# Experts' weights in rows of 8 and 4 KB, the residual in the matching channel order, and a held-back sum

## The chip, the cores and the metric

The kernel runs on one core of one Trainium2 chip, in one launch. The metric is the device time in microseconds (us). A core has five engines that run beside each other: TensorE (PE, matrix products into the PSUM banks, with its weight loads listed as PEld), VectorE (DVE), ScalarE (ACT), GpSimd (POOL) and SyncE (SP, which here issues the DMAs). [...]

## What is computed

One layer of a hybrid diffusion block on 512 latent tokens and 256 context tokens of 2048 channels, all in float32. Ahead of the part that matters here stand a modulated norm, one input projection, three kinds of heads and the output projection w_out with the gated residual. Then:

```python
hl = _rmsnorm(xl, g_ffn) * (1.0 + s2_l) + sh2_l
f = _hier_moe(hl, ...)        # top-1 of 4 groups, top-2 of its 8 experts; 32 experts
#   per expert e:  (silu(h @ w1[e]) * (h @ w3[e])) @ w2[e],  w1, w3: 2048 x 512,  w2: 512 x 2048
xl = xl + ga2_l * f
return _rmsnorm(xl, g_final)
```

The weights of one expert are three matrices of 4.19 MB; all 32 experts' are read once.

## The kernel before, in words

The whole program up to the end of the experts is in an order written out by hand: each engine works through its instructions in program order, and a tile's buffer is given out again once its last reader in program order has been issued. PSUM has eight banks (line 57): four with the tag `mm`, which from line 1205 on are the `held` banks for the rest of the kernel, and four with the tag `bg`, from which `bank()` takes one for a short time.

**The residual.** `out_tile` (line 868) finishes one of 16 tiles of 128 channels of the output projection: DVE adds the gated residual, TensorE transposes the tile (`xtr`) and adds to the router's logits, ACT copies the transposed tile into `xr` (128 tokens on the partitions, 4 token tiles, 2048 channels in natural order) and takes the squares. The last tile (line 886) shares this between ACT and DVE.

**The experts** go in 16 pairs (`expert_pair`, line 1385), two experts side by side in the two column halves of TensorE. `gather` (line 1308) fetches the tokens of four experts, so of two pairs: it splits `xr` into high and low parts (`token_parts`, ACT copies, DVE subtracts), multiplies them with a one-hot matrix in 16 steps (four channel groups of four token tiles; the fourth step of a group is followed by four DVE evacuations `hg`, line 1348, and the next group's first step writes the same two `held` banks). The steps are dealt out over the second pair of each four experts by `STEPS` (line 43), through `steps(n)`.

In a pair, w1 and w3 are multiplied in four column groups of four channel tiles each; behind the first group stands what is in `late`. Then DVE multiplies the two results (line 1427), TensorE transposes them (`pt`), ACT copies them (`at`), and `down` multiplies with w2 in four runs of 512 columns, each into one `held` bank, alternating. After each run DVE scales it (`ys`, line 1451), `split` makes a high and a low part (ACT line 128, DVE line 129), and `combine` (line 1370) is put in `late`: for four token tiles, two products into a bank `pc`, and a DVE addition into the running residual `xf` (line 1381). It runs behind the next run's products, the last run's behind the first group of the next pair's w1.

**The weights.** `wseq` lists tiles of 1 MB in the order of use: two channel tiles of both experts for w1 and w3, two row tiles of both experts and 512 columns for w2, all in rows of 2 KB, each tile by two DMAs of 512 KB (line 1113). SP issues them as buffers come free; in the steady state there are ten (six of `wpool`, one of `moe`, three of `mixs`). `next_w` gives back the tile used before, issues what fits, and takes the next.

Of the kernel before, what the change touches and what calls it, by code (L numbers as in the profile page):

```python
# [50 lines left out]
def hybrid_block_kernel(ctx: ExitStack, tc: tile.TileContext, I, out):  # L51
# [419 lines left out]
    def cc(c):  # L471
        return slice(128 * c, 128 * c + 128)
# [395 lines left out]
    def out_tile(dt, po):  # L868

        xt = ob["xt"].pop(dt)  # L870
        if dt == KT - 1:
            nc.scalar.copy(ob["logs"][0][TWO[0]], pl["log"][TWO[0]])
        nc.vector.scalar_tensor_tensor(xt, po, ga1[:, dt:dt + 1], xt, op0=ALU.mult, op1=ALU.add)
        yield
        if dt == 0:
            pl["log"] = bank("plog")
        pt = bank("xtr")
        for t in range(4):
            nc.tensor.transpose(pt[:, cc(t)], xt[:, cc(t)], ident)
        waiting.append((dt, xt))  # L880
        while waiting and (dt % 2 or dt == KT - 2):
            k, x_ = waiting.popleft()
            sl = TWO[k % 2]
            nc.tensor.matmul(pl["log"][sl], ob["wrs"][:, k], x_, start=k < 2, stop=k >= KT - 2,
                             tile_position=(0, sl.start))
        if dt == KT - 1:

            rows = pt.rearrange("p (t d) -> p t d", t=4)
# [3 lines left out]
            nc.vector.tensor_copy(xr[:, 2:4, cc(dt)], rows[:, 2:4])  # L892
            for t in (2, 3):
                x_ = xr[:, t, cc(dt)]
                nc.vector.tensor_tensor_reduce(sqs[t], x_, x_, 1.0, 0.0, op0=ALU.mult, op1=ALU.add,
                                               accum_out=ob["ssq"][:, t, dt:dt + 1])
            nc.scalar.copy(ob["logs"][0][TWO[1]], pl["log"][TWO[1]])
            nc.scalar.copy(xr[:, 0:2, cc(dt)], rows[:, 0:2])
            return
        nc.scalar.copy(xr[:, :, cc(dt)], pt.rearrange("p (t d) -> p t d", t=4))  # L900
        for t in range(4):
            sq = ob["pool"].tile([P, P], F32, name="sq", tag="sq", bufs=4)
            nc.scalar.activation(sq, xr[:, t, cc(dt)], AF.Square, accum_out=ob["ssq"][:, t, dt:dt + 1])
            if t == 1:
                yield
        yield
# [99 lines left out]
    def four(which, name, dtype=F32):  # L1006

        return mixs.tile([P, 4, 512], dtype, name=name, tag=f"m{which}")

    def split_mix(*at):  # L1010

        for n in at:
            q, m = n // 4, MIX_ORDER[n]
            if n % 4 == 0:
                halves[q] = [four(2 * q + j, "mx", F32R) for j in range(2)]
            mh[m], ml[m] = (t[:, n % 4] for t in halves[q])
            nc.scalar.copy(mh[m], mix[m])
            (nc.gpsimd if 4 <= n < 15 else nc.vector).tensor_tensor(ml[m], mix[m], mh[m].bitcast(F32), op=ALU.subtract)  # L1018

    def open_out():  # L1020
# [39 lines left out]

        ob["constant"] = constant()

    def load_xt(dt):
        xt = ob["xt"][dt] = ob["pool"].tile([P, T], F32, name="xt", tag="xt", bufs=6)
        nc.sync.dma_start(xt, I["xT"][dt])


    def rows(t, k, n):

        return t[:, 0:2 * k * n // 512].rearrange("p a (b n) -> p (a b) n", n=n).rearrange("p (e k) n -> p e k n", e=2)  # L1070

    wseq = deque()

    def add(name, e, k, nk, o, n):
        v = I[name][e:e + 2].rearrange("e (k p) n -> p e k n", p=P)
        wseq.append((nk, n, v[:, :, k:k + nk, o:o + n]))

    for e in range(0, NE, 2):
        for name in ("w1", "w3"):
            for k in range(0, KT, 2):  # L1080
                add(name, e, k, 2, 0, 512)
        for c in range(4):
            if e < NE - 2 or c < 3:
# [15 lines left out]
    def load_weights(n=1000):  # L1099
        while places and wseq and n:  # L1100
            n -= 1
            at = places.popleft()
            if at not in until or total - len(wseq) < until[at]:
                nk, c, v = wseq.popleft()
                if at == "w":
                    w = ob["wpool"].tile([P, 4, 512], F32, name="w", tag="w")
                elif at == "m":
                    w = moe.tile([P, 4, 512], F32, name="wm", tag="wm")
                else:
                    w = four(at, "w")  # L1110
                w = rows(w, nk, c)
                for j in range(2):
                    nc.sync.dma_start(w[:, j], v[:, j])
                wtiles.append((w, at))

    def next_w():

        places.extend(used)
        used.clear()
        load_weights()  # L1120
        w, at = wtiles.popleft()
        used.append(at)
        return w

    def beside_out(i, n):
        run(jobs, n)
# [177 lines left out]
    def prod():  # L1304
        turn.rotate()
        return turn[0]

    def gather(g):
# [12 lines left out]
        for n in range(16):  # L1321
# [22 lines left out]
            if t == 3:  # L1344
                for i in range(4):
                    k = 4 * c + i
                    h = moe.tile([P, 256], F32, name="hg", tag="hg", bufs=16)
                    nc.vector.scalar_tensor_tensor(h, pg[i], A2[:, k:k + 1], norm, op0=ALU.mult, op1=ALU.mult)
                    nc.scalar.activation(h, h, AF.Identity, bias=B2[:, k:k + 1])  # L1349
                    hs.append(h)  # L1350
            yield

    xf = {}
    late = deque()
    fs = keep.tile([P, 4, 5], F32, name="fs")

    def square(t, i, x):
# [11 lines left out]

    def combine(oht, c, o, n, hl, last=False, ts=range(4)):  # L1370

        x = xf.get(c)
        if x is None:
            x = xr[:, :, 512 * c:512 * c + 512]
            xf[c] = four(1 + c, "xf")
        for t in ts:
            pc = bank("pc")
            for m, y in enumerate(hl):
                nc.tensor.matmul(pc[:, 0:n], oht[:, cc(t)], y[:, 0:n], start=m == 0, stop=m == 1)  # L1379
            x_ = xf[c][:, t, o:o + n]  # L1380
            nc.vector.tensor_tensor(x_, pc[:, 0:n], x[:, t, o:o + n], op=ALU.add)  # L1381
            if last:
                square(t, c + o // 256, x_)

    def expert_pair(e, oh, hs):
        last = e == NE - 2
# [3 lines left out]
        for name in ("w1", "w3"):  # L1390
            acc = prod()
            for c in range(4):
                if name == "w1" and e == 0:

                    steps(FIRST[c])
                for k in range(4 * c, 4 * c + 4):
                    if k % 2 == 0:
                        w = next_w()
                    for j in range(2):
                        nc.tensor.matmul(acc[64 * j:64 * j + 64], hs[k][:, sl + 64 * j:sl + 64 * j + 64], w[:, j, k % 2],  # L1400
                                         start=k == 0, stop=k == KT - 1, tile_position=(0, 64 * j))
# [46 lines left out]
        def scaled(pd, c, o, n):  # L1448
# [2 lines left out]
            nc.vector.scalar_tensor_tensor(ys, pd, tw[:, 1:2], ga2b[:, 512 * c + o:512 * c + o + n], op0=ALU.mult, op1=ALU.mult)  # L1451
            return ys

        if not last:
# [79 lines left out]
    with tc.If(flag > 0):  # L1534
# [3 lines left out]
        hT = ov.tile([P, KT, T], F32, name="hT")  # L1538
        for t in range(4):
            y = big([D], "y")  # L1540
            nc.scalar.mul(y, xr[:, t], rst[:, t:t + 1])
# [171 lines left out]
```

## Time and profile before

| | |
|---|---|
| median of 3 runs | 2288.06 us (2285.24 to 2288.96) |
| the profiled execution | 2293.04 us |
| its span, first to last instruction | 2291.3 us |
| its granted clock, mean | 0.99 |
| TensorE busy / DVE / ACT / POOL | 96% / 54% / 30% / 12% |
| DMA moved | 600.81 MB, mean 262 GB/s |

Up to about 1230 us run the projections and heads, from about 1248 to 2272 us the experts, then the last norm and the store. The busy shares are means over stages of different kinds, so the stretch of the experts is read by itself, in windows. A wait is idle time of an engine, put down to what ended it. The DMA share can pass 1, since packets of one engine overlap.

### The profile page before, as it was taken

Reading aid. Unit: us, or ns where it says so; the run is one execution under the profiler, and the core shown is the slowest. Engines: PE = TensorE matmul, PEld = TensorE weight load, DVE = VectorE, ACT = ScalarE, POOL = GpSimd, SP = SyncE. Lnnn points to the kernel's source line nnn. Section 1 sums busy time; section 2 is a strip of 40 time slices with the busy share of each in tenths; the row PEclk is TensorE's granted clock in tenths of the full one; section 3 lists DMA queues with packets and bytes.
Section 4 is the critical chain, followed back from the end, with each engine's and each line's share of the span. In section 5 each row is a group of like instructions: output and inputs, shape, how many; then the busy total and the mean of one; then the engine's idle time right before and its main releaser. Section 6 shows DMA issues by size and latency. Waiting matters only on the chain. (4 is left out here: it accounts for less than half of the span.)

```text
span 2291.3 us, 32501 instructions
## 1 busy us (share of the span) xinstructions
PE 2191.1 (96%) x12151; PEld 1414.7 (62%) x12151; DVE 1245.8 (54%) x2201; ACT 692.4 (30%) x1400; POOL 268.3 (12%) x323
## 2 busy tenths in 40 slices
PE   7989999999999999999998999999999999999996
PEld 4667888888877887877776444444435344444433
DVE  4468668868777666645555333434434343434424
ACT  4344232332444445452334121211202021211202
POOL 0033414405122121122000000000000000000000
PEclk9999999999999999999999999999999999999998
DMA  9964222222346555536974999999999999999996
GB/s 342 370 205 138 75 92 70 84 88 86 112 147 176 174 174 164 167 93 200 303 262 168 328 344 369 403 380 404 381 404 382 390 403 380 403 381 404 381 404 261
DMA packets 321234, 600.81 MB, mean 262 GB/s; under 512 B 25392, under 2 KB 35376, under 8 KB 321072
## 3 DMA queue, kind: packets, MB, share of 16 engines
q1 hardware_dynamic: 317232, 593.44, 72.3%
q0 software_dynamic: 3840, 5.25, 1.1%
q8 instruction: 97, 1.59, 0.3%
q14 instruction: 65, 0.53, 0.1%
HBM read 589.15 MB, written 4.19 MB: 259 GB/s over the span
## 5 line engine op out<-in xcount | busy, mean ns | idle before, releaser
L209 PE MATMUL p<-xh,wh 128*128 128x512 f32 (+1 forms) x1184 | 417.0, 365 | 4.3 <-ACT wh L128 2.1
L1400 PE MATMUL held<-w,hg 128*64 128x512 f32 x1848 | 416.2, 596 | 1.2 <-ACT hg L1349 0.6
L210 PE MATMUL p<-xl,wh 128*128 128x512 f32 (+1 forms) x1184 | 399.5, 354 | 0.0
L1400 PEld LDWEIGHTS held<-w,hg 128*64 128x64 f32 x1848 | 126.8, 137 | 239.2 <-issue 214.1
L129 DVE TENSOR_TENSOR wl<-w,wh 128x512 fp32r<-128x512 f32 x216 | 176.5, 817 | 160.4 <-ACT wh L128 144.8
L212 PE MATMUL p<-xh,wl 128*128 128x512 f32 (+1 forms) x1184 | 254.2, 352 | 5.6 <-DVE wl L129 5.6
L209 PEld LDWEIGHTS p<-xh,wh 128*128 128x128 f32 x1184 | 223.9, 189 | 46.1 <-issue 5.6
L210 PEld LDWEIGHTS p<-xl,wh 128*128 128x128 f32 x1184 | 224.1, 189 | 34.1 <-issue 1.4
L128 ACT CAST wh<-w 128x512 fp32r<-128x512 f32 x216 | 133.6, 619 | 317.4 <-PE p L210 219.1
L1444 PE MATMUL held<-w,at 128*64 128x512 f32 (+1 forms) x944 | 213.6, 595 | 10.9 <-ACT at L1434 10.9
L212 PEld LDWEIGHTS p<-xh,wl 128*128 128x128 f32 x1184 | 191.4, 189 | 35.1 <-DVE wl L129 7.9
L1381 DVE TENSOR_TENSOR xf<-pc,xf 128x512 f32<-128x512 f32 (+1 forms) x244 | 149.6, 674 | 50.9 <-PE pc L1379 50.8
L1191 DVE TENSOR_TENSOR parts<-xr,parts 128x512 fp32r<-128x512 f32 x112 | 76.9, 691 | 167.8 <-ACT parts L1190 167.8
L1332 PEld LDWEIGHTS held<-oh,parts 128*128 128x128 f32 x896 | 111.5, 188 | 67.2 <-issue 46.9
L369 DVE SCALAR_TENSOR_TENSOR m_acc<-w_ada,sc,m_acc 128x512 f32<-128x512 f32 x180 | 145.5, 809 | 10.7 <-DMA w_ada<-w_ada 8.4
L1444 PEld LDWEIGHTS held<-w,at 128*64 128x64 f32 x944 | 63.1, 137 | 128.5 <-issue 104.2
L1332 PE MATMUL held<-oh,parts 128*128 128x256 f32 x896 | 128.4, 289 | 14.4 <-ACT hg L1349 10.3
L1190 ACT CAST parts<-xr 128x512 fp32r<-128x512 f32 x112 | 68.5, 618 | 167.5 <-PE held L1332 166.6
L128 ACT CAST wh<-ys 128x512 fp32r<-128x512 f32 x60 | 37.1, 618 | 255.2 <-DVE ys L1451 147.5
L209 PE MATMUL po<-mx,wh 128*128 128x512 f32 x256 | 105.3, 411 | 2.3 <-ACT wh L128 1.6
L1379 PE MATMUL pc<-wh,oht 128*128 128x512 f32 (+1 forms) x260 | 105.7, 407 | 0.0
L210 PE MATMUL po<-mx,wh 128*128 128x512 f32 x256 | 102.9, 402 | 0.3 <-DVE mx L1018 0.2
(359 smaller groups left out, 2823.5 us busy)
## 6 DMA issues: line engine op xcount, KB each, us to landing
w<-w SPq DMA_DIRECT2D x692, 512.0 KB
w_ada<-w_ada SPq DMA_DIRECT2D x384, 256.0 KB
w<-w_in SPq DMA_DIRECT2D x184, 256.0 KB
wm<-w SPq DMA_DIRECT2D x74, 512.0 KB
w<-w_out SPq DMA_DIRECT2D x64, 256.0 KB
w_st<-w_st SPq DMA_DIRECT2D x32, 192.0 KB
x<-xT SPq DMA_DIRECT2D x16, 256.0 KB
xt<-xT SPq DMA_DIRECT2D x16, 256.0 KB
```

The source lines that it names most:

```text
L128: nc.scalar.copy(wh, w)
L129: nc.vector.tensor_sub(wl, w, wh.bitcast(F32))
L209: nc.tensor.matmul(po, h, mh_, start=first, stop=False)
L210: nc.tensor.matmul(po, h, ml_, start=False, stop=False)
L212: nc.tensor.matmul(po, l, mh_, start=False, stop=last)
L369: nc.vector.scalar_tensor_tensor(accs[j], loads.popleft(), s, accs[j], op0=ALU.mult, op1=ALU.add)
L1191: engine.tensor_tensor(l, x_, h.bitcast(F32), op=ALU.subtract)
L1332: nc.tensor.matmul(pg[i], y[:, cc(i)], oh[:, t], start=t == 0 and m == 0 and i % 2 == 0, stop=t == 3 and m == 1 and i % 2 == 1)
L1379: nc.tensor.matmul(pc[:, 0:n], oht[:, cc(t)], y[:, 0:n], start=m == 0, stop=m == 1)
L1381: nc.vector.tensor_tensor(x_, pc[:, 0:n], x[:, t, o:o + n], op=ALU.add)
L1400: nc.tensor.matmul(acc[64 * j:64 * j + 64], hs[k][:, sl + 64 * j:sl + 64 * j + 64], w[:, j, k % 2], start=k == 0, stop=k == KT - 1, tile_p ...
L1444: nc.tensor.matmul(pd[64 * j:64 * j + 64, 0:n], at[:, 128 * f + 64 * j:128 * f + 64 * j + 64], w[:, j, f - f0], start=f == 0, stop=f == 3, ...
```

## The change

1. w1 and w3 are read expert by expert in runs of 512 channels: partition p takes the four consecutive rows 4p to 4p + 3, one row of 8 KB in HBM, a whole tile of 1 MB in one DMA. So channel tile i of a run now holds the channels 4p + i. w2 is read in tiles of one row tile, both experts, 1024 columns: rows of 4 KB.
2. The residual `xr` is written in that order (`spread`), so the gather's parts have the matching channels; the first addition of each column run puts it back in natural order (`in_order`), as does the branch for overflowing tokens. The shift and gain are permuted once, by 16 small products with columns of the identity.
3. `next_w(2)` takes both experts' tiles at once. `down_two` multiplies two column runs beside each other: runs 0 and 1 in the `held` banks, runs 2 and 3 in two `bg` banks. The gather's steps of two runs follow each other. The last pair keeps `down`.
4. Behind each of the first column groups at most one entry of `late` runs. The combination of run 3 goes to `fill` and is done at the next pair's change from w3 to w2: two token tiles ahead of the transposes and two behind them.

The core of the diff:

```diff
-        nc.scalar.copy(xr[:, :, cc(dt)], pt.rearrange("p (t d) -> p t d", t=4))
+        for t in range(4):
+            nc.scalar.copy(spread(dt)[:, t], pt[:, cc(t)].rearrange("p (q i) -> p i q", i=4))
...
+        pq = bank("pq")
+        for m in range(4):
+            for i in range(4):
+                nc.tensor.matmul(pq[32 * m:32 * m + 32, 0:2 * KT].rearrange("p (w g i) -> p w g i", w=2, i=4)[:, :, :, i],
+                                 ident[:, i::4], mods[:, 3:5, m::4, 0], start=True, stop=True, tile_position=(0, 32 * m))
+        nc.vector.tensor_copy(mods[:, 3:5, :, 1], pq[:, 0:2 * KT].rearrange("p (w k) -> p w k", w=2))
...
+    def add_run(name, e, c):
+        wseq.append((0, 0, I[name][e, 512 * c:512 * c + 512].rearrange("(p k) n -> p k n", p=P)))
...
-            for k in range(0, KT, 2):
-                add(name, e, k, 2, 0, 512)
+            for c in range(4):
+                for j in range(2):
+                    add_run(name, e + j, c)
+        if e < NE - 2:
+            for c in (0, 2):
+                for k in range(4):
+                    add("w2", e, k, 1, 512 * c, 1024)
+            continue
...
+            if (c, t) not in begun:
+                begun.add((c, t))
+                natural = lambda y: y.rearrange("p (q i) -> p q i", i=4)
+                nc.vector.tensor_tensor(natural(x_), natural(pc), in_order(xr[:, t, 512 * c:512 * c + 512]), op=ALU.add)
+            else:
+                nc.vector.tensor_tensor(x_, pc[:, 0:n], x_, op=ALU.add)
...
+                ws = next_w(2)
...
-                while late:
+                if late:
                     late.popleft()()
...
         nc.vector.tensor_mul(a, gu[1], a)
+        filler((0, 1))
...
         nc.scalar.copy(at, pt)
+        filler((2, 3))
...
+        def down_two(c0):
+            pds = [prod(), prod()] if not c0 else [bank("pd"), bank("pd")]
+            for f in range(4):
+                w = next_w()
+                for pd, cs in zip(pds, (slice(0, 512), slice(512, 1024))):
+                    for j in range(2):
+                        nc.tensor.matmul(pd[64 * j:64 * j + 64], at[:, 128 * f + 64 * j:128 * f + 64 * j + 64],
+                                         w[:, j, 0, cs], start=f == 0, stop=f == 3, tile_position=(0, 64 * j))
+            return pds
...
-            for c in range(4):
-                pd = down(c, 0, 512)
+            for c0 in (0, 2):
+                pds = down_two(c0)
                 if ahead:
-                    steps(STEPS[6 + c])
+                    steps(STEPS[6 + c0] + STEPS[7 + c0])
                 while late:
                     late.popleft()()
-                hl = split(scaled(pd, c, 0, 512))
-                late.append(lambda ts=range(4), c=c, hl=hl: combine(oht, c, 0, 512, hl, ts=ts))
+                for c, pd in zip((c0, c0 + 1), pds):
+                    hl = split(scaled(pd, c, 0, 512))
+                    if c < 3:
+                        late.append(lambda c=c, hl=hl: combine(oht, c, 0, 512, hl))
+                    else:
+                        fill.append(lambda ts, hl=hl: combine(oht, 3, 0, 512, hl, ts=ts))
```

## Rows read from the trace of the kernel before

**Rows 1.** The page, part 1: busy us (share of the span) x instructions.
```profile
PE 2191.1 (96%) x12151; PEld 1414.7 (62%) x12151; DVE 1245.8 (54%) x2201; ACT 692.4 (30%) x1400; POOL 268.3 (12%) x323
```

**Rows 2.** Windows: PE, PEld, DVE, ACT, POOL busy us (instructions), clock, DMA share, GB/s.
```profile
1510.00:1520.00 10.00, 10.00 (x53) 5.81 (x53) 7.00 (x12) 0.87 (x2) 0.00 (x0) 1.00 0.99 349
...
1550.00:1560.00 10.00, 10.00 (x45) 4.10 (x42) 5.28 (x8) 1.23 (x2) 0.00 (x0) 1.00 1.05 408
1529.50:1657.81 128.31, 123.59 (x610) 57.41 (x608) 52.22 (x94) 24.19 (x45) 0.00 (x0) 1.00 1.04 393
```

**Rows 3.** TensorE's waits, 1255 to 2245 us: us in total, times, longest.
```profile
PE pt L1432 <- DVE act L1427: 10.9, 16, 0.9
PE held L1332 <- ACT hg L1349: 10.3, 7, 1.5
PE held L1444 <- ACT at L1434: 10.2, 15, 0.7
PE held L1332 <- DVE parts L1191: 4.1, 14, 0.3
PE held L1400 <- ACT hg L1349: 0.6, 1, 0.6
PE held L1400 <- DMA w<-w: 0.6, 2, 0.3
```

**Rows 4.** Timeline at a change to w2: start, us, engine, line [idle before].
```profile
1544.58 0.69 DVE L1427 TENSOR_TENSOR act<-held,act 128x512 f32<-128x512 f32 x1 [13.06 <-PE held L1400]
1545.33 0.66 PE L1432 MATMUL pt<-cf,act 128*128 128x128 f32 x4 [0.87 <-DVE act L1427]
1546.02 0.58 ACT L1434 COPY at<-pt 128x512 f32<-128x512 f32 x1 [15.81 <-PE pt L1432]
1546.66 7.09 PE L1444 MATMUL held<-w,at 128*64 128x512 f32 x32 [0.68 <-ACT at L1434]
```

**Rows 5.** Timeline of one combination behind a w2 run.
```profile
1553.68 0.50 PE L1379 MATMUL pc<-wh,oht 128*128 128x512 f32 x1
1554.02 0.39 PE L1379 MATMUL pc<-wl,oht 128*128 128x512 f32 x1
1554.25 0.40 PE L1379 MATMUL pc<-wh,oht 128*128 128x512 f32 x1
1554.45 2.48 DVE L1381 TENSOR_TENSOR xf<-pc,xf 128x512 f32<-128x512 f32 x4 [1.91 <-PE pc L1379]
...
1555.72 1.94 PE L1444 MATMUL held<-w,at 128*64 128x512 f32 x8
```

**Rows 6.** Timeline of gather steps 11 (1619.72) and 12 (1624.44).
```profile
1619.72 1.20 PE L1332 MATMUL held<-oh,parts 128*128 128x256 f32 x8
1620.85 0.62 ACT L1190 CAST parts<-xr 128x512 fp32r<-128x512 f32 x1 [4.76 <-PE held L1332]
1620.86 3.65 PE L1444 MATMUL held<-w,at 128*64 128x512 f32 x16
...
1622.11 1.65 DVE L1348 SCALAR_TENSOR_TENSOR hg<-held,mods,norm 128x256 f32<-128x256 f32 x4
...
1624.44 1.21 PE L1332 MATMUL held<-oh,parts 128*128 128x256 f32 x8
...
1625.49 0.39 PE L1379 MATMUL pc<-wh,oht 128*128 128x512 f32 x1
```

**Rows 7.** Timeline of the output projection's end.
```profile
1221.98 0.56 ACT L900 COPY xr<-xtr 128x512 f32<-128x512 f32 x1
...
1224.38 1.05 PE L884 MATMUL plog<-xt,wrs 128*36 128x512 f32 x2 [1.13 <-ACT logs L872]
```

**Rows 8.** An ACT copy of 128 columns out of PSUM: ns min/median/max.
```profile
L379 ACT COPY rows<-sums x16: 243/266/273, 236.8 to 1197.8; 128x128 f32<-128x128 f32 x16
```

**Rows 9.** Timeline: eight small instructions of TensorE.
```profile
1197.29 0.43 PE L376 MATMUL sums<-m_acc,cf 128*32 128x128 f32 x8
```

**Rows 10.** Timeline: a strided reduction; line 1381: the first additions, ns.
```profile
1063.35 1.18 DVE L1054 TENSOR_REDUCE ws<-wr 128x36 f32<-128x576 f32 x1
...
L1381 DVE TENSOR_TENSOR xf<-pc,xr x16: 680/681/692, 1297.7 to 1316.4; 128x512 f32<-128x512 f32 x16
```

More of the change, by code (lines that the diff above doesn't have):

```diff
@@ L886, in out_tile @@
         if dt == KT - 1:
-            rows = pt.rearrange("p (t d) -> p t d", t=4)
+            rows, to = pt.rearrange("p (t q i) -> p t i q", t=4, i=4), spread(dt)
             sqs = [ob["pool"].tile([P, P], F32, name="sq", tag="sq", bufs=4) for _ in range(4)]
@@ L891, in out_tile @@
                 nc.scalar.activation(sqs[t], pt[:, cc(t)], AF.Square, accum_out=ob["ssq"][:, t, dt:dt + 1])
-            nc.vector.tensor_copy(xr[:, 2:4, cc(dt)], rows[:, 2:4])
             for t in (2, 3):
-                x_ = xr[:, t, cc(dt)]
-                nc.vector.tensor_tensor_reduce(sqs[t], x_, x_, 1.0, 0.0, op0=ALU.mult, op1=ALU.add,
+                nc.vector.tensor_copy(to[:, t], rows[:, t])
+            for t in (2, 3):
+                x_ = to[:, t]
+                nc.vector.tensor_tensor_reduce(sqs[t].rearrange("p (i q) -> p i q", i=4), x_, x_, 1.0, 0.0, op0=ALU.mult, op1=ALU.add,
                                                accum_out=ob["ssq"][:, t, dt:dt + 1])
             nc.scalar.copy(ob["logs"][0][TWO[1]], pl["log"][TWO[1]])
-            nc.scalar.copy(xr[:, 0:2, cc(dt)], rows[:, 0:2])
+            for t in (0, 1):
+                nc.scalar.copy(to[:, t], rows[:, t])
             return
-        nc.scalar.copy(xr[:, :, cc(dt)], pt.rearrange("p (t d) -> p t d", t=4))
+        for t in range(4):
+            nc.scalar.copy(spread(dt)[:, t], pt[:, cc(t)].rearrange("p (q i) -> p i q", i=4))
         for t in range(4):
             sq = ob["pool"].tile([P, P], F32, name="sq", tag="sq", bufs=4)
-            nc.scalar.activation(sq, xr[:, t, cc(dt)], AF.Square, accum_out=ob["ssq"][:, t, dt:dt + 1])
+            nc.scalar.activation(sq.rearrange("p (i q) -> p i q", i=4), spread(dt)[:, t], AF.Square,
+                                 accum_out=ob["ssq"][:, t, dt:dt + 1])
             if t == 1:
@@ L1008, in four, with spread, in_order @@
         return mixs.tile([P, 4, 512], dtype, name=name, tag=f"m{which}")
+    def spread(dt):
+        c, m = dt // 4, dt % 4
+        return xr[:, :, 512 * c:512 * c + 512].rearrange("p t (i m q) -> p t m i q", i=4, m=4)[:, :, m]
+    def in_order(x):
+        return x.rearrange("p (i q) -> p q i", i=4)
     def split_mix(*at):
@@ L1110, in load_weights, with next_w @@
                     w = four(at, "w")
-                w = rows(w, nk, c)
-                for j in range(2):
-                    nc.sync.dma_start(w[:, j], v[:, j])
+                if nk:
+                    w = rows(w, nk, c)
+                    for j in range(2):
+                        nc.sync.dma_start(w[:, j], v[:, j])
+                else:
+                    nc.sync.dma_start(w, v)
                 wtiles.append((w, at))
-    def next_w():
+    def next_w(n=1):
         places.extend(used)
@@ L1120, in next_w @@
         load_weights()
-        w, at = wtiles.popleft()
-        used.append(at)
-        return w
+        ws = []
+        for _ in range(n):
+            w, at = wtiles.popleft()
+            used.append(at)
+            ws.append(w)
+        return ws if n > 1 else ws[0]
     def beside_out(i, n):
@@ L1347, in gather @@
                     h = moe.tile([P, 256], F32, name="hg", tag="hg", bufs=16)
-                    nc.vector.scalar_tensor_tensor(h, pg[i], A2[:, k:k + 1], norm, op0=ALU.mult, op1=ALU.mult)
-                    nc.scalar.activation(h, h, AF.Identity, bias=B2[:, k:k + 1])
+                    nc.vector.scalar_tensor_tensor(h, pg[i], mods[:, 4, k, 1:2], norm, op0=ALU.mult, op1=ALU.mult)
+                    nc.scalar.activation(h, h, AF.Identity, bias=mods[:, 3, k, 1:2])
                     hs.append(h)
@@ L1353, in hybrid_block_kernel @@
     xf = {}
-    late = deque()
+    late, fill, begun = deque(), deque(), set()
     fs = keep.tile([P, 4, 5], F32, name="fs")
@@ L1370, in combine @@
     def combine(oht, c, o, n, hl, last=False, ts=range(4)):
-        x = xf.get(c)
-        if x is None:
-            x = xr[:, :, 512 * c:512 * c + 512]
+        if c not in xf:
             xf[c] = four(1 + c, "xf")
@@ L1380, in combine, with filler @@
             x_ = xf[c][:, t, o:o + n]
-            nc.vector.tensor_tensor(x_, pc[:, 0:n], x[:, t, o:o + n], op=ALU.add)
+            if (c, t) not in begun:
[4 more added lines that the diff above has]
+                nc.vector.tensor_tensor(x_, pc[:, 0:n], x_, op=ALU.add)
             if last:
                 square(t, c + o // 256, x_)
+    def filler(ts):
+        if fill:
+            fill[0](ts)
+            if 3 in ts:
+                fill.popleft()
     def expert_pair(e, oh, hs):
@@ L1395, in expert_pair @@
                     steps(FIRST[c])
+                ws = next_w(2)
                 for k in range(4 * c, 4 * c + 4):
-                    if k % 2 == 0:
-                        w = next_w()
                     for j in range(2):
-                        nc.tensor.matmul(acc[64 * j:64 * j + 64], hs[k][:, sl + 64 * j:sl + 64 * j + 64], w[:, j, k % 2],
+                        nc.tensor.matmul(acc[64 * j:64 * j + 64], hs[k][:, sl + 64 * j:sl + 64 * j + 64], ws[j][:, k % 4],
                                          start=k == 0, stop=k == KT - 1, tile_position=(0, 64 * j))
-                while late:
+                if late:
                     late.popleft()()
@@ L1452, in scaled @@
             return ys
+        def down_two(c0):
[3 more added lines that the diff above has]
+                for pd, cs in zip(pds, (slice(0, 512), slice(512, 1024))):
+                    for j in range(2):
+                        nc.tensor.matmul(pd[64 * j:64 * j + 64], at[:, 128 * f + 64 * j:128 * f + 64 * j + 64],
+                                         w[:, j, 0, cs], start=f == 0, stop=f == 3, tile_position=(0, 64 * j))
+            return pds
         if not last:
-            for c in range(4):
-                pd = down(c, 0, 512)
+            for c0 in (0, 2):
+                pds = down_two(c0)
                 if ahead:
-                    steps(STEPS[6 + c])
+                    steps(STEPS[6 + c0] + STEPS[7 + c0])
                 while late:
                     late.popleft()()
-                hl = split(scaled(pd, c, 0, 512))
-                late.append(lambda ts=range(4), c=c, hl=hl: combine(oht, c, 0, 512, hl, ts=ts))
+                for c, pd in zip((c0, c0 + 1), pds):
+                    hl = split(scaled(pd, c, 0, 512))
+                    if c < 3:
+                        late.append(lambda c=c, hl=hl: combine(oht, c, 0, 512, hl))
+                    else:
+                        fill.append(lambda ts, hl=hl: combine(oht, 3, 0, 512, hl, ts=ts))
             return
@@ L1540, in hybrid_block_kernel @@
             y = big([D], "y")
-            nc.scalar.mul(y, xr[:, t], rst[:, t:t + 1])
+            for c in range(4):
+                sl = slice(512 * c, 512 * c + 512)
+                nc.scalar.mul(y[:, sl].rearrange("p (q i) -> p q i", i=4), in_order(xr[:, t, sl]), rst[:, t:t + 1])
             for k in range(KT):
```

3 lines of the change are left out of this document (1 added, 2 removed).

## The prediction

> **What bounds the kernel now.** Read the page's busy shares first: TensorE is busy 96% of the span [rows 1]. That number alone proves nothing, so go to the table by stretch. From 1529.50 to 1657.81 us four experts pass (two passes of `expert_pair`, the second with the next gather in it). TensorE is busy 123.59 of 128.31 us, and the DMA engines show a share of 1.04 and 393 GB/s [rows 2]. Both look full, so ask which of the two waits. The stream runs at 408 GB/s in an ordinary 10 us, but at 349 where all weight buffers are full and TensorE is still busy [rows 2]: it has about 4% to spare. The list of TensorE's own waits in the expert stage settles it. Of 36.7 us, weights account for 0.6 us; the rest is 10.9 us for the product with the gate (DVE, L1427), 10.2 us for the transposed copy (ACT, L1434), 10.3 us for the evacuation of the gather's banks and 4.7 us of smaller ones [rows 3]. So TensorE's own order of work is the bound, the stream is close behind it, and only what lengthens or shortens TensorE's row counts.
>
> **The change, part by part.**
>
> *Long rows.* w1 and w3 arrive as one DMA of 1 MB with rows of 8 KB in place of two of 512 KB with rows of 2 KB, w2 in rows of 4 KB. TensorE waits 0.6 us for weights in the whole stage [rows 3], so even a faster stream gives at most that: I take 0. The cover is the buffered lead; what it costs if that goes, and what the rows would give if the stream were the pace, are two of the rivals.
>
> *The held-back sum.* At each change from w3 to w2 TensorE stands idle twice: 0.87 us until DVE has multiplied, then, after four transposes, 0.68 us until ACT has copied them [rows 4]. The change puts the last column run's combination of the pair before (eight products, 2.04 us from 1553.68 to 1555.72 in a like place [rows 5]) into these two holes, half and half: about 1 us before the transposes and 1 us behind them. Both halves are as long as their holes. All of it goes but in the first pair, which has nothing held back: 10.9 + 10.2 us [rows 3], 0.7 more for the last pair's second hole, which lies behind that window, less 1.6 for the first pair: **-20.2 us**.
>
> *Fewer turns between kinds of product.* A combination of eight products takes 2.04 us where eight times their pitch of 0.2325 (1554.02 to 1554.25 [rows 5]) is 1.86: each such block costs 0.18. Per pair four blocks become two (two merge, one goes into the holes): 2 x 0.18 x 15 = **-5.4 us**.
>
> *Two runs at a time, and their banks.* `down_two` holds two accumulators. For runs 0 and 1 these are the `held` banks; for runs 2 and 3 they come from the four `bg` banks and stay taken until `scaled`, which is issued behind the combinations of runs 0 and 1. So those eight sums go through two banks and not four. From the rows: a sum is two products 0.23 apart; DVE starts its addition 0.43 after the second one starts (1554.02 to 1554.45), four additions take 2.48, so 0.62 each [rows 5], and TensorE goes on 0.06 after a DVE end (1545.27 to 1545.33 [rows 4]). A bank is therefore free again 0.23 + 0.43 + 0.62 + 0.06 = 1.34 us after its sum began. Two sums go off in 1.34 where four banks allow two in 0.93. Over the three rounds that wait this is 1.23, and the first round's slower first product adds up to 0.1: 1.3 us a pair, 15 pairs: **+19.5 us**. Bounds: 1.1 if DVE alone paces (the eighth sum waits for six additions), 1.45 if DVE is late: 17 to 22. Behind the waiting products on TensorE stand the next pair's w1 products, which nothing else holds up.
>
> *Two gather steps in a row.* `steps(STEPS[6] + STEPS[7])` runs steps 11 and 12 back to back. Step 12 opens the next four channel tiles and writes the banks that step 11 has just filled, so it waits for DVE's four evacuations (`hg`). Before, a whole w2 run of 3.6 us stood between. The rows show what it waits for: step 11 ends at 1620.86, ACT copies a part until 1621.47, DVE subtracts, and only then evacuates, 1622.11 to 1623.76 [rows 6]. The first two evacuations free the first bank at 1622.94, four products follow (half of the 1.05 us from 1624.44 to 1625.49 [rows 6]) until 1623.5, and the other four start at 1623.82 and end at 1624.35, where they would have ended at 1621.91. That is 2.44 us in each of the seven pairs with a gather: **+17.1 us**. The same wait at step 4, behind step 3, already costs 1.5 seven times [rows 3]. Lower bound, if DVE began at once: 1.35, so 9.5; upper 19.
>
> *The residual in channel order.* Each of the 16 output tiles now needs four ACT copies of 128 columns (0.27 each [rows 8]) where one of 512 took 0.56 [rows 7]: +0.5 a tile. Beside w_out's products that is hidden, but at its end ACT is the late one: TensorE waits 1.13 us for ACT's logits, behind the copies and squares of two tiles [rows 7]. So two tiles count, 1.0, and 0.2 for DVE's second copy in the last tile: **+1.2 us**. Should strided access be slower, the strided reduction (1.18 us for 576 columns, 2.05 ns each) against the ordinary addition (681 ns for 512, 1.33 ns each) [rows 10] bounds it at 1.5 times: 2.4 here, and up to 3 in the first pair's sixteen strided additions, of which I take nothing.
>
> *The permuted shift and gain.* 16 tiny products, 32 instructions; eight of like size took 0.43 us [rows 9], so 1.7 at most, and 0 if a wait of that stage swallows them: **+0.8 us**.
>
> Sum: -20.2 - 5.4 + 19.5 + 17.1 + 1.2 + 0.8 = **+13.0 us**. The profiled execution took 2293.04 us (span 2291.3, 1.7 around it), 5.0 above the median of 2288.06; it would become 2306.0, and the median **2301**. With all the low ends (17, 9.5, 0.5, 0) the sum is +1.4, with the high ends (22, 19, 5.4, 1.7 and holes filled to nine tenths) about +25: 2289 to 2313.
>
> **The rivals.**
>
> *Faster: the two new waits do not decide.* This needs sums that leave their banks as fast as TensorE makes them: it decides once a bank's turn is under 0.93 us against the 1.34 above, and once the evacuation ends within step 11's own 1.05 us. For it speaks that DVE is busy only 52.22 of 128.31 us [rows 2]; against it that both waits are latencies in a fixed order and not load. Then only -20.2 - 5.4 + 2.0 remains: 2264. If one of the two is gone and the other stays, 2301 - 19.5 = 2282 or 2301 - 17.1 = 2284, on either side of the smallest difference that can be told.
>
> *The stream is the pace after all.* Then TensorE's holes are slack, and the stage goes as the bytes do: the 402.7 MB of the experts' weights (32 x 3 x 4.19) from 1025 us at 393 GB/s to 987 at 408 [rows 2], -38: 2250. For it speaks the share of 1.04, against it the 0.6 us [rows 3]. [...]
>
> *The stream falls behind.* `next_w(2)` wants both experts' tiles before the first product, so the second is needed 1.7 us earlier (eight products at 0.213), and both are given back together. The two waits for weights of 0.3 us at the stage's end [rows 3] show that the lead can reach zero. If faster rows don't give it back, each four experts lose up to 2 us at the tightest place, seven or eight times: +14 on the sum, 2315. Against it: TensorE's new waits come in the same cycle and give the stream time.
>
> *It does not do what it says.* If the stream stays at 408 GB/s in ordinary stretches, the long rows did nothing for bandwidth; the time is then the forecast's, since TensorE is not waiting for it.
>
> **How the numbers follow.** The forecast, both waits in force, has 0.56 (0.06 of it so low that it cannot be told from no change); one of the two gone 0.22, half of it on each side of that bound; both gone 0.09; the stream as the pace 0.03; the stream behind 0.10. About 0.2%, 4.6 us, is what a measurement of this kernel can tell from no change. Faster: 0.09 + 0.03 + 0.11 = 0.23. Same: 0.06 + 0.11 = 0.17. Slower: 0.50 + 0.10 = 0.60. The range leaves out the cases with both waits gone and with the stream as the pace, and the upper half of the case where it falls behind, 0.17 together: 2278 to 2314.
>
> **What would show it.** Right: TensorE's waits at L1427 and L1434's consumers fall to the first pair's; new waits of TensorE at `pc` for DVE's additions, about 1.3 us per pair; step 12 starting 2.4 us late behind `hg` in seven pairs; four experts taking 130 us; DMA packets down from 317232 to under 200000. Wrong: no wait at `pc` although two banks serve it; four experts in 125 us; waits for weights of over 5 us in all; or TensorE's products themselves at another pitch.

## The result, and the profile after

The changed kernel takes **2309.37 us** in the median of 4 runs (2308.60 to 2311.01), the kernel before, beside it, 2288.51 us (2285.24 to 2293.35). The ratio is 1.0085 with a 95% interval from 1.0072 to 1.0099: slower by 20.9 us, where +13.0 was forecast. 2309 lies inside the forecast range.

Three lines of the page after (busy us, share, instructions; then packets) answer [rows 1]:

```profile
PE 2198.3 (95%) x12183; PEld 1410.9 (61%) x12183; DVE 1253.7 (54%) x2203; ACT 693.9 (30%) x1446; POOL 268.0 (12%) x323
DMA packets 188113, 600.79 MB, mean 260 GB/s; under 512 B 21296, under 2 KB 31280, under 8 KB 155184
q1 hardware_dynamic: 184112, 593.43, 69.1%
```

The same bytes go in 184112 packets where it was 317232. The windows of the changed kernel (columns as in [rows 2]: stretch, length, busy PE, PEld, DVE, ACT, POOL, granted clock, DMA share, GB/s): four experts, four experts again, an ordinary 10 us, 10 us with full buffers, and 3.4 us in a pair with a gather.

```profile
1533.50:1665.70 132.20, 125.56 (x610) 57.96 (x608) 52.52 (x94) 24.21 (x45) 0.00 (x0) 0.99 0.95 381
1797.40:1927.60 130.20, 124.45 (x611) 56.99 (x609) 52.43 (x94) 24.21 (x45) 0.00 (x0) 1.00 0.96 387
1560.00:1570.00 10.00, 9.15 (x39) 3.56 (x35) 4.56 (x7) 0.62 (x1) 0.00 (x0) 1.00 1.02 431
1650.00:1660.00 10.00, 10.00 (x50) 4.83 (x48) 6.08 (x11) 2.32 (x5) 0.00 (x0) 1.00 0.63 211
1630.20:1633.60 3.40, 3.22 (x12) 2.32 (x14) 1.52 (x5) 2.10 (x5) 0.00 (x0) 0.50 1.00 424
```

The long rows did what they say: the stream's own pace in its fastest 10 us rose from 408 to 431 GB/s. It brought nothing: the stream stands still longer instead (211 GB/s with full buffers, where it was 349 [rows 2]), and four experts take 130.2 us, not 128.3. The last row is the one that nothing in the prediction speaks of: TensorE at a granted clock of 0.50, half of the 1.00 that the ordinary 10 us have. The granted clock is the share of TensorE's full clock that the profile lists; "half clock" below stands for 0.50.

TensorE's waits from 1255 to 2265 us of the changed kernel (total us, times, longest), beside [rows 3]:

```profile
PE held L1368 <- DVE hg L1384: 14.7, 7, 2.1
PE pc L1413 <- DVE xf L1420: 11.9, 42, 0.3
PE held L1368 <- ACT hg L1385: 10.3, 7, 1.5
PE held L1444 <- DMA w<-w: 2.9, 3, 1.4
PE pt L1478 <- DVE act L1472: 2.4, 8, 0.9
PE held L1368 <- DVE parts L1227: 1.8, 7, 0.3
PE pc L1413 <- DVE xf L1418: 1.8, 6, 0.7
PE held L1508 <- ACT at L1480: 0.7, 1, 0.7
```

The two old holes fell from 10.9 and 10.2 us to 2.4 and 0.7, and both new waits are there: step 12 for the evacuation (14.7) and the sums for their banks (11.9 + 1.8). The three places in the timeline (start, duration, instruction, idle before). First a change from w3 to w2, which answers [rows 4] (w2 cut at the end of the view):

```profile
1548.35 0.50 PE L1413 MATMUL pc<-wh,oht 128*128 128x512 f32 x1
1549.38 0.60 PE L1478 MATMUL pt<-cf,act 128*128 128x128 f32 x4
1549.74 0.48 PE L1413 MATMUL pc<-wh,oht 128*128 128x512 f32 x1
1550.85 1.51 PE L1508 MATMUL held<-w,at 128*64 128x512 f32 x6
```

No idle time is left: four products, the transposes, four products, w2. Then the eight sums of runs 0 and 1, beside [rows 5]:

```profile
1564.73 0.50 PE L1413 MATMUL pc<-wh,oht 128*128 128x512 f32 x1
1565.50 1.29 DVE L1420 TENSOR_TENSOR xf<-pc,xf 128x512 f32<-128x512 f32 x2 [4.07 <-PE pc L1413]
1566.24 0.50 PE L1413 MATMUL pc<-wh,oht 128*128 128x512 f32 x1 [0.31 <-DVE xf L1420]
1567.86 0.47 PE L1413 MATMUL pc<-wh,oht 128*128 128x512 f32 x1 [0.28 <-DVE xf L1420]
1569.35 0.50 PE L1413 MATMUL pc<-wh,oht 128*128 128x512 f32 x1 [0.25 <-DVE xf L1420]
1570.61 3.65 PE L1444 MATMUL held<-w,hg 128*64 128x512 f32 x16
```

A pair of sums starts every 1.5 to 1.6 us, and the block of sixteen products takes 5.88 us (1564.73 to 1570.61) where two blocks of 2.04 [rows 5] were 4.1. Last, steps 11 and 12, beside [rows 6] (the last group is cut at the end of the view):

```profile
1627.08 1.20 PE L1368 MATMUL held<-oh,parts 128*128 128x256 f32 x8
1628.20 0.62 ACT L1226 CAST parts<-xr 128x512 fp32r<-128x512 f32 x1 [8.37 <-PE held L1368]
1629.46 1.65 DVE L1384 SCALAR_TENSOR_TENSOR hg<-held,mods,norm 128x256 f32<-128x256 f32 x4
1630.38 2.08 PE L1368 MATMUL held<-oh,parts 128*128 128x256 f32 x8 [2.10 <-DVE hg L1384]
1632.39 2.11 PE L1508 MATMUL pd<-w,at 128*64 128x512 f32 x6
```

Step 12 waits 2.10 us, and then its eight products take 2.08 us where step 11's took 1.20: the row at clock 0.50 above is this place. Five such stretches of 3.4 us, at a granted clock of 0.50 to 0.51, lie in the expert stage, at 1367.4, 1500.5, 1630.2, 1763.3 and 2026.2 us, each in a pair with a gather; they begin between 0.2 us before and 2.0 us after the end of step 12's wait. The profiled execution before has one stretch there.

### The profile page after: what moved, and what is told of

Read it like the earlier page. It is cut to its first block, busy times and chain, and to the rows that moved or that the text cites. A ratio compares the mean times of both kernels' runs of the same rounds, so it can differ in the third digit from the quotient of the medians.

```text
span 2307.9 us, 32399 instructions
## 1 busy us (share of the span) xinstructions
PE 2198.3 (95%) x12183; PEld 1410.9 (61%) x12183; DVE 1253.7 (54%) x2203; ACT 693.9 (30%) x1446; POOL 268.0 (12%) x323
## 2 busy tenths in 40 slices
DMA packets 188113, 600.79 MB, mean 260 GB/s; under 512 B 21296, under 2 KB 31280, under 8 KB 155184
## 3 DMA queue, kind: packets, MB, share of 16 engines
q1 hardware_dynamic: 184112, 593.43, 69.1%
## 5 line engine op out<-in xcount | busy, mean ns | idle before, releaser
L1444 PE MATMUL held<-w,hg 128*64 128x512 f32 x1848 | 456.3, 596 | 3.6 <-DMA w<-w 2.9
L1444 PEld LDWEIGHTS held<-w,hg 128*64 128x64 f32 x1848 | 140.7, 137 | 266.3 <-issue 253.9
L1368 PE MATMUL held<-oh,parts 128*128 128x256 f32 x896 | 129.0, 290 | 27.1 <-DVE hg L1384 14.7
L1413 PE MATMUL pc<-wh,oht 128*128 128x512 f32 (+1 forms) x260 | 115.1, 443 | 13.7 <-DVE xf L1420 11.9
L1508 PE MATMUL pd<-w,at 128*64 128x512 f32 x432 | 102.6, 627 | 0.0
L1413 PE MATMUL pc<-wl,oht 128*128 128x512 f32 (+1 forms) x260 | 101.7, 392 | 0.1
```

The source lines that it names most:

```text
L1368: nc.tensor.matmul(pg[i], y[:, cc(i)], oh[:, t], start=t == 0 and m == 0 and i % 2 == 0, stop=t == 3 and m == 1 and i % 2 == 1)
L1508: nc.tensor.matmul(pd[64 * j:64 * j + 64], at[:, 128 * f + 64 * j:128 * f + 64 * j + 64], w[:, j, 0, cs], start=f == 0, stop=f == 3, tile_ ...
```

## The experiments

All times are medians, each beside runs of the kernel before on the same chip.

| kernel | us | ratio to before, 95% |
|---|---|---|
| changed | 2309.4 | 1.0085 (1.0072 to 1.0099) |
| e1 step 11 early | 2307.0 | 1.0070 (1.0053 to 1.0087) |
| e2 own banks | 2303.8 | 1.0055 (1.0038 to 1.0072) |
| e3 both | 2305.2 | 1.0057 (1.0040 to 1.0073) |
| e9 step 11 behind | 2283.7 | 0.9973 (0.9962 to 0.9984) |
| e10 behind, own banks | 2276.8 | 0.9944 (0.9924 to 0.9965) |
| e13 busy wait | 2303.1 | 1.0062 (1.0048 to 1.0075) |
| e6 the wait in before | 2313.8 | 1.0096 (1.0075 to 1.0117) |
| e5 rows alone | 2291.0 | 1.0000 (0.9989 to 1.0012) |
| e4 held-back sum alone | 2269.0 | 0.9910 (0.9893 to 0.9926) |
| e8 rows, held-back sum | 2272.1 | 0.9923 (0.9904 to 0.9942) |
| e11 held-back sum, steps | 2266.4 | 0.9895 (0.9878 to 0.9913) |
| e12 rows, held-back sum, steps | 2259.2 | 0.9860 (0.9841 to 0.9879) |

**e1: step 12 without its wait, first try.**

```diff
-STEPS = (0, 3, 3, 2, 2, 1, 1, 1, 1, 1, 1, 0, 0)
+STEPS = (0, 3, 3, 2, 2, 2, 1, 0, 1, 1, 1, 0, 0)
```

> The changed kernel with gather step 11 done before the transposes, so that step 12 stands alone behind the first two column runs of w2; nothing else differs. Theory (TensorE's own order sets the pace, and step 12's wait for the evacuations behind step 11 is one of the two new costs): the seven waits of 2.1 us go, 15 us, and if the five stretches at half the granted clock that begin in this wait come from it, 1.7 us each of them too: 2286 us. If the clock stretches have another cause: 2295. Rival (the weight stream or something else would take up the time): the wait turns up at the weights' semaphores, 2305 to 2310.

2307.0 us: hardly anything. Neither theory named the place. The timeline of e1 shows it:

```profile
1623.63 1.65 DVE L1384 SCALAR_TENSOR_TENSOR hg<-held,mods,norm 128x256 f32<-128x256 f32 x4
1624.14 1.70 ACT L1385 ACTIVATE hg<-hg,mods 128x256 f32<-128x256 f32 x4 [1.41 <-DVE hg L1384]
1625.76 0.56 ACT L1480 COPY at<-pt 128x512 f32<-128x512 f32 x1
1626.37 1.94 PE L1508 MATMUL held<-w,at 128*64 128x512 f32 x8 [2.81 <-ACT at L1480]
```

Step 11's four ACT instructions now stand in ACT's queue ahead of the copy `at`, so w2 waits for them. TensorE's wait for the copy in e1:

```profile
PE held L1508 <- ACT at L1480: 21.2, 8, 3.6
```

Seven of the eight waits are new, 2.8 to 3.6 us long, in exchange for the 14.7. A step has two tails, the four evacuations on DVE and the four ACT instructions behind them; the edit moved TensorE's part past one consumer and put the tails in front of another. Only two of the seven waits are followed by a stretch at half clock.

**e2 and e3: four banks for the sums, and both edits.**

```diff
-            pds = [prod(), prod()] if not c0 else [bank("pd"), bank("pd")]
+            pds = [prod(), prod()] if not c0 else [bank("pd"), bank("pd")] if ahead else held[2:]
```

> The changed kernel in which the 8 of 15 pairs without a gather take column runs 2 and 3 into the two gather banks, which are idle then; the sums of runs 0 and 1 have all four banks again there. Theory: in a traced pair eight such sums take 5.9 us where they would take 3.9 with banks free, so 8 x 2.0 = 16 us go: 2293 us, and TensorE's waits at pc for DVE's additions fall from 13.7 us to 6.5. Rival (DVE's additions, 0.65 us each, are the pace and not the banks): the wait stays in another place, less than 6 us gained.

2303.8 us, 7 us less (1.0085 to 1.0055) and not 16. TensorE's waits at `pc` for DVE's additions in e2:

```profile
PE pc L1413 <- DVE xf L1420: 6.0, 21, 0.3
PE pc L1413 <- DVE xf L1418: 0.6, 3, 0.2
```

They halved as expected, from 13.7 to 6.6 us. From the first `pa` product of a pair to that of the next, the pairs without a gather take 51.4 us at best where it was 53.2, and the eight of them 11.0 us less in sum. So the banks were the cause and not DVE. But the seven pairs with a gather take 3.1 us more in sum: six of them now have a stretch at half clock, where it was five.

> Both edits of the two kernels above in one. Theory: the gains add up, 23 + 16 us: 2270 us (2264 to 2280), faster than the kernel before. Rival (the stream is close behind TensorE's order): part of the gain comes back as waits for weights, over 5 us of them, and the time stays above 2280.

2305.2 us. Both theories fell, the first because of e1's own new wait: the 21.2 us at `at` stand in e3 too, here with a stretch at half clock in each of its seven pairs with a gather.

**e9: step 11 where its tails are in nobody's way.** Behind the copy `at` and the held-back products, ahead of w2:

```diff
-STEPS = (0, 3, 3, 2, 2, 1, 1, 1, 1, 1, 1, 0, 0)
+STEPS = (0, 3, 3, 2, 2, 1, 1, 0, 1, 1, 1, 0, 0)
...
         filler((2, 3))
+        if ahead:
+            steps(1)
```

> The changed kernel with gather step 11 done behind the transposed copy and the second half of the held-back sum, ahead of w2; step 12 stays behind the first two column runs. Its evacuations then stand ahead of nothing that TensorE needs soon. Theory: the seven waits of 2.1 us are gone without a successor, 14.7 us, and with them the five stretches at half the granted clock, 1.7 us each: 2286 us (2283 to 2290). If those stretches have another cause: 2295. Rival (the weight stream is close behind): the gain comes back as waits for weights, 2298 to 2308, weights over 10 us in all.

2283.7 us, within the theory's 2283 to 2290 and 25.6 us below the changed kernel (1.0085 to 0.9973). TensorE's waits in the same stretch of e9:

```profile
PE pc L1413 <- DVE xf L1420: 11.9, 42, 0.3
PE held L1368 <- ACT hg L1385: 10.3, 7, 1.5
PE held L1444 <- DMA w<-w: 2.5, 3, 1.4
```

The 14.7 us are gone, weights stay at 2.5, and no stretch of the expert stage is at half clock. A pair with a gather takes 74.25 us instead of 76.9 or, with the stretch, about 78.6. (The third one takes 75.2 and 79.0: in both kernels TensorE waits 0.9 us for a weight tile there.)

**e10: e9 with e2's banks.**

> The kernel above, and column runs 2 and 3 of the eight pairs without a gather in the idle gather banks. Theory: the two gains add, the second one as measured alone in those pairs' own periods (11 us): 2275 us (2270 to 2280), below the kernel before. Rival (the stream): 2285 or more, with waits for weights of over 10 us.

2276.8 us, 7 us below e9, 4 less than the 11 foretold for it. The pairs without a gather gained 10.8 us in sum; the pairs with one lost 1.6 and the end 1.9. In five of the seven pairs with a gather w1's and w3's products stand longer, 28.4 to 29.1 us where it was 28.37 in all, and weights are up to 4.1 us in four waits: the stream, now at 397 to 402 GB/s over four experts, is coming up behind. That the tenths too are waits for weights wasn't shown.

**e6: the wait alone, in the kernel before.**

```diff
-STEPS = (0, 3, 3, 2, 2, 1, 1, 1, 1, 1, 1, 0, 0)
+STEPS = (0, 3, 3, 2, 2, 1, 2, 0, 1, 1, 1, 0, 0)
```

> The kernel before with one number changed: gather steps 11 and 12 run back to back behind the first column run of w2, in seven pairs. Theory: TensorE waits 2.1 us and is late by 2.4 in each, 17 us: 2307 us; if the wait also brings the stretches at half the granted clock, 1.7 us for each of them, up to 2319. Rival (the wait only takes up slack): 2290 us.

2313.8 us, +23.6. The row of TensorE's wait in e6, and the window of one of its stretches:

```profile
PE held L1332 <- DVE hg L1348: 14.7, 7, 2.1
```

```profile
1761.60:1765.00 3.40, 3.40 (x11) 1.09 (x11) 1.80 (x3) 1.29 (x3) 0.00 (x0) 0.50 0.98 371
```

Pairs with a gather take 77.20 to 77.22 us in three cases, 74.78 + 2.42, and 78.85 to 78.94 in the four that have a stretch at half clock: 7 x 2.42 + 4 x 1.67 = 23.6. One gather step moved in `STEPS` costs as much, with the old rows and the old banks, as the whole change does on balance.

**e13: the same wait, but TensorE works through it.**

```diff
-                    steps(STEPS[6 + c0] + STEPS[7 + c0])
+                    steps(1)
+                    dm, o_ = bank("dm"), slots[0]
+                    for i in range(16):
+                        nc.tensor.matmul(dm[:, 0:256], o_[:, 0, 0:128], o_[:, 0], start=True, stop=True)
+                    steps(1)
```

(for c0 = 0; the condition around it is left out here)

> The changed kernel with sixteen products of 128x256 that nobody reads put between gather steps 11 and 12 in the seven gather pairs: step 12 waits for its banks as before, but TensorE works through the wait instead of standing still. Their results are used nowhere. Theory (the stretches at half the granted clock come of TensorE standing still for 2.1 us here): the order of everything else keeps its times, the five stretches are gone, 5 x 1.7 us: 2301 us (2299 to 2304). Rival (they come of something else, or at random): 2307 to 2312 us, and stretches at half clock still in the gather pairs.

2303.1 us. TensorE's wait before step 12 in e13, and the window of the 3.5 us behind one of them:

```profile
PE held L1368 <- DVE hg L1384: 1.3, 7, 0.2
```

```profile
1624.50:1628.00 3.50, 3.45 (x19) 1.58 (x20) 1.69 (x3) 1.88 (x5) 0.00 (x0) 1.00 0.97 410
```

No stretch of the expert stage is at half clock, and six of the seven pairs with a gather take 76.9 us, what the changed kernel's two undisturbed ones take; the order costs the same, only the standing still is gone. So the stretches come of TensorE's idle 2.1 us. By the ratios they cost 5 us (1.0085 to 1.0062), by the traces 7.7 us over the seven pairs with a gather (547.2 against 539.5). What decides which of the seven waits is followed by one stays open: e1's are longer, and only two of them are.

**e5, e4, e8: the parts alone.** e5 is the change without `down_two`, `fill` and w2's long rows; e4 is the kernel before with the held-back sum (`fill`) alone; e8 is e5 with `fill`. The line that holds the sum back, in e4 against the kernel before (the two calls of `filler` are as in the change, and e8 has the same new line):

```diff
-                late.append(lambda ts=range(4), c=c, hl=hl: combine(oht, c, 0, 512, hl, ts=ts))
+                (fill if c == 3 else late).append(lambda ts=range(4), c=c, hl=hl: combine(oht, c, 0, 512, hl, ts=ts))
```

> The changed kernel with w2 again in rows of 2 KB, one column run at a time, no held-back sum and the steps where they were: what is left of the change is w1 and w3 in DMAs of 1 MB with rows of 8 KB, the residual in the matching channel order and the permuted shift and gain. Theory (TensorE doesn't wait for the stream): only the small costs of the order stay, 2290 to 2294 us. Rival 1 (the stream sets part of the pace): faster rows give 2270 or less. Rival 2 (two tiles wanted at once run the buffers dry): 2300 or more, with waits for weights of over 10 us.

> The kernel before with one edit: the combination of the last column run is held back and put half before the transposes, half behind them, as in the change; weight rows, residual order, w2 runs and gather steps stay as before. Theory: the waits for the gate's product and for the transposed copy go in 14 of 15 pairs, 20.2 us, and one turn between kinds of product per pair, 2.7: 2266 us. Rival (these holes were the stream's slack): 2280 to 2290, with waits for weights in their place.

> The kernel with the long rows of w1 and w3 and the channel order alone, and the held-back sum added; w2 stays one column run at a time in rows of 2 KB. Theory: the two effects add, 2291 - 21 = 2270 us, and since the held-back sum alone left the stream no pause (404 GB/s over four experts, DMA share 1.05 in every 10 us), faster rows save the 0.3 to 0.5 us that its gather pairs lost: 2266 to 2270. Rival (the rows cost something of their own once TensorE is faster): 2273 or more.

e5: 2291.0 us, no difference that can be told. e4: 2269.0, -20.7, near the theory. e8: 2272.1, 2 us above its range, and whether rows help or cost here can't be told at 0.9923 against 0.9910. In the traces the first pair, where the strided additions are, takes 2.1 us more in e8 than in e4 (53.5 against 51.4). A window of four experts in e4 shows what has become scarce:

```profile
1896.48:2021.57 125.09, 123.16 (x610) 57.74 (x608) 52.12 (x94) 24.21 (x45) 0.00 (x0) 1.00 1.05 403
```

403 GB/s over four whole experts, where in [rows 2] it was 393 with pauses: with the holes filled, the rows of 2 KB run without a pause at the pace that they had between pauses.

**e11 and e12: what long rows are worth then.** In both, other numbers of gather steps take away the wait at step 4; e11 on top of e4, e12 on top of e8:

```diff
-STEPS = (0, 3, 3, 2, 2, 1, 1, 1, 1, 1, 1, 0, 0)
+STEPS = (0, 2, 2, 4, 1, 1, 2, 1, 1, 1, 1, 0, 0)
```

> The kernel before with the held-back sum and other numbers of gather steps (2, 2, 4 and 1 in w3, then 1, 2, 1, 1, 1 and 1), so that step 3 ends a group and step 4 no longer waits 1.5 us for its evacuation. Theory (the stream now is the pace: four experts' 50.33 MB at 404 GB/s take 124.6 us, and they take 124.8 already): what TensorE gains it loses again to weights, 2265 to 2269 us. Rival (TensorE's order is still the pace): seven times 1.5 us less up to 0.6 for parts, 2260 us or less.

> The same other numbers of steps on top of the long rows of w1 and w3 with the held-back sum. Theory: the stream has room here (418 to 427 GB/s where it isn't held up by full buffers), so TensorE's gain stays: 2256 to 2262 us, below the same kernel with rows of 2 KB by 5 or more. Rival (rows make no difference to the pace): the time of the kernel with rows of 2 KB within 3 us.

e11 2266.4, e12 2259.2 us. The window of four experts in e11, TensorE's waits for weights in e11's expert stage, then windows of four experts and of 10 us in e12:

```profile
1888.87:2013.89 125.02, 124.19 (x610) 57.93 (x608) 52.14 (x94) 24.21 (x45) 0.00 (x0) 1.00 1.05 402
```

```profile
PE held L1407 <- DMA w<-w: 2.6, 11, 0.3
```

```profile
1891.26:2015.01 123.75, 123.22 (x611) 58.93 (x609) 52.12 (x94) 24.21 (x45) 0.00 (x0) 1.00 1.01 407
1820.00:1830.00 10.00, 10.00 (x55) 4.99 (x54) 4.79 (x12) 2.57 (x5) 0.00 (x0) 1.00 1.00 424
```

The same edit brings 13 to 14 us with long rows (2272.1 to 2259.2, 0.9923 to 0.9860) and 3 with short ones (0.9910 to 0.9895), which can't be told from nothing: in e11 four experts still take what 50.3 MB take at 402 GB/s, 125.2 us. Counted from each product's start to the next one's, the edit takes 13.2 us off the gather in e11 (against e4) and 13.5 in e12 (against e8); w1's and w3's products take back 10.8 of it in e11 and 0.4 in e12. The list names 2.6 us of waits for weights in e11; that the rest is the stream too follows from the 402 GB/s and isn't shown wait by wait. That is the rival "the stream is the pace after all", false for the kernel before and true for its successor. e12 beats both kernels, by 1.4% and 2.2%.

## Why the prediction was right, and where not

The direction and the two mechanisms held; e9, e10 and e6 show each by itself. The sizes, in the two profiled executions, from the first pair's `pa` to the last pair's (953.64 us before, 974.78 after):

| term | forecast | measured | from |
|---|---|---|---|
| held-back sum | -20.2 | -28.6 | 14 pairs x 1.90, first pair 2.0 |
| fewer turns | -5.4 | -4.5 | w2's 64 products 14.19 to 13.88 us, 15 pairs |
| two banks | +19.5 | +26.9 | the 32 products of the sums: 8.15 to 10.06 us in 8 pairs, 8.00 to 9.66 (e9) in 7 |
| steps 11 and 12 | +17.1 | +18.8 | 7 x (76.93 in e13 - 74.25 in e9) |
| half clock | none | +6.0 | the pairs with a gather, 547.2 against 539.5 in e13; less the 1.7 of the one stretch before |
| long rows (weights) | 0 | +0.9 | one wait in the third pair with a gather |
| strided first sums | 0 (0 to 3) | +1.4 | what is left in the first pair |
| sum | +11.0 | +20.9 | the trace: +21.1 |

The other two terms, +2.0 together, lie ahead of this stretch. The times of products here run from each start to the next instruction's start, so a wait counts to the product before it; 1.4 is worked out as a remainder, of the first pair alone.

- *Held-back sum*: right in kind, 8 us too small. The step that failed is "both halves are as long as their holes", with holes of 0.87 and 0.68 read as idle time [rows 4]. From start to start the two pieces shrank by 0.93 and 0.97. For the second, the idle time counts from the listed end of the transposes, but the next product starts before it: at 1549.74, 0.36 after the first of four transposes that are listed until 1549.98. And in the pairs with a gather the first half also covers TensorE's wait of 0.3 for the parts ahead of step 10: the waits for parts were 4.1 us in 14 places [rows 3] and are 1.8 in 7. Alone (e4) it brings 20.7 in medians and 26.2 over this stretch of the traces, 1.7 of it the half clock of before; the end, from the last `pa` on, takes 2.8 us longer there (67.8 against 64.9).
- *Banks*: right in kind, 7 us too small. The round was put at 1.34 us and is 1.5 to 1.6: additions take 0.645 and not 0.62 (1.29 for two), and the first product after a wait is followed 0.31 to 0.34 later by its second, not 0.23. This error and that of the held-back sum all but cancel, so part of the forecast's nearness is luck.
- *Steps 11 and 12*: 2.44 a pair was forecast, e6 gives 2.42, the changed kernel 2.68. This was the forecast's best number.
- *Half clock*: this is what is missing. The wait of 2.1 us was priced as lost time alone; it costs up to 1.7 more where TensorE, just before or within 2 us after its end, runs at a granted clock of 0.50 for 3.4 us. The row was there to be asked about: the trace of before has such a stretch, and that pair took 76.45 us instead of 74.78:

```profile
1744.50:1747.90 3.40, 3.40 (x8) 0.98 (x10) 0.00 (x0) 0.00 (x0) 0.00 (x0) 0.51 1.06 410
```

- *Residual order, shift and gain*: +2.0 forecast; e5 gives +0.8 with an interval of about 2.7 either way, the strided first sums included. At w_out's end the second ACT tile counts less than thought; TensorE waits 1.24 us for the logits there, 1.13 before [rows 7].
- *Strided first sums*: the bound of 1.5 from [rows 10] was the value, and nothing was taken for it. In e5, which has them without `down_two`, the first pair is 3.1 us longer than before (56.69 against 53.58), at the bound of 3; in the changed kernel 1.4 are left. The two groups after (us in all, mean ns):

```profile
L1418 DVE TENSOR_TENSOR xf<-pc,xr 128x512 f32<-128x512 f32 x16 | 15.8, 1049 | 4.2 <-PE pc L1413 4.2
L1420 DVE TENSOR_TENSOR xf<-pc,xf 128x512 f32<-128x512 f32 x236 | 150.5, 684 | 41.1 <-PE pc L1413 39.9
```

- *Long rows 0*: right but for 2.9 us of waits for weights, under the 5 that would have spoken against it. The lead ran out three times: 0.9 us in the third pair with a gather, 0.7 and 1.4 in the last pair.
- *The rivals*: neither of the new waits was absent or hidden, so the faster cases fell; the stream neither set the pace nor, but for those 2.9 us, fell behind in the changed kernel, and it did do what it says. Eight products with w3 in a row, which the prediction took as 8 x 0.213, take 1.72 us in the trace of before (1535.71 to 1537.43), so 0.215 each. Of the signs that were named, the fallen waits, the packets (188113) and the two new waits are there, and four experts take the 130 us foretold where no stretch is at half clock (130.2), 132.2 where one is.

In medians the loss is 20.9 us. The spans of the two profiled executions differ by 16.6: the changed one reaches its first `pa` 4.7 us earlier (1268.0 against 1272.7). The one before has 17.1 us at half clock between 1060 and 1245 us, against 3.4. In e11, where this part of the kernel is as before and the same stretches are 3.4 us too, the first `pa` stands at 1267.6, so this looks like the clock's doing and not the change's.

## What to carry to other kernels

Filling a hole with work from elsewhere paid here (e4); what ate the gain were the other parts of the same change, the two accumulators of w2's longer rows, which took the banks, and the two gather steps in a row, which lost the distance between them. So look what the rest of the loop turns on before two runs are merged. Before a step is moved, list all its instructions on all engines: the tails that it leaves on DVE and ACT decide where it may stand (e1 against e9). And a faster stream was worth nothing while TensorE's order was the pace (e5) and 7 us once that order had been shortened (e12 against e11), so measure it on the improved order.

## What the runs showed of the hardware

- TensorE standing still for 2.1 us was followed by 3.4 us at a granted clock of 0.50 in 5 of 7 such places in the changed kernel, in 6 of 7 in e2 and in 4 of 7 in e6, and in none of 7 where it worked through the same 2.1 us (e13). The length of the wait doesn't settle it: of seven waits of 2.8 to 3.6 us each in e1 and e3, 2 and 7 were followed by such a stretch, and the one in the expert stage before began behind three short waits (0.33, 0.45 and 0.68 us between 1741.3 and 1744.5). Waits of 0.3 us at the banks, three in each pair, brought none in e9.
- DMAs of 1 MB with rows of 8 KB beside ones of 512 KB with rows of 4 KB run at 419 to 431 GB/s in the changed kernel's ordinary 10 us; rows of 2 KB, with no pause in e4, at 396 to 408.
- An addition on DVE that reads one operand as float32 at a distance of 512 bytes (`in_order`) takes 1049 ns in the changed kernel instead of the 684 of the ordinary one, 1.53 times as long. What makes it slower wasn't tested.
